# One HGRN2 chunk at a time against chunks in pairs: level products of 256 tokens in two PSUM banks, the banks shared out anew

## The chip, the cores and the metric

The kernel runs on one core of one Trainium2 chip. The metric is the device time of one execution in microseconds (us), as the median over several runs. Five engines work side by side, each through its own instructions in order: TensorE (PE; PEld is its weight load), VectorE (DVE), ScalarE (ACT), GpSimd (POOL) and SyncE (SP), which issues nearly all DMAs. Products are written to PSUM, which has eight banks of 512 fp32 values per partition.

## The reference

One layer of a hybrid trunk: 1024 tokens and 16 meta tokens ahead of them, width 1024. One input projection feeds three mixers, whose outputs (384 + 384 + 256 wide) go through one output projection, a layer norm, a squared-ReLU MLP (hidden width 4096) and a second layer norm. The change touches the first mixer, HGRN2, with 6 heads of 64:

```python
zf = f_raw;  q = silu(q_raw);  v = i_raw
log_f = logaddexp(log_sigmoid(zf), log(lb) + log_sigmoid(-zf))     # log of the forget gate
k = (1 - lb) * sigmoid(-zf)
# per chunk, with G = cumsum(log_f) over the tokens of the chunk
o_inter = (q * exp(G)) @ state
scores[t, s] = sum_k q[t, k] * exp(G[t, k] - G[s, k]) * k[s, k]     # s <= t
o = o_inter + scores @ v
state = exp(G_last) * state + (k * exp(G_last - G)).T @ v
...
o = rms_norm(o) * norm_w * silu(g_raw)
h = layer_norm(ALPHA * h + concat(y_a, y_b, y_c) @ w_out)
ff = square(relu(h @ w_mlp_in)) @ w_mlp_out
h = layer_norm(ALPHA * h + ff)
```

## The kernel before

**Precision and products.** Most products are "three-part" ones: `mm3` (L107 to L110) splits each fp32 operand into a rounded `hi` (ScalarE, L100) and the rest `lo` (VectorE, L87) and issues hi x hi, lo x hi and hi x lo. The small products of the mixers are plain fp32 and take two passes each on PE.

**Order.** The kernel is a list of units (Python functions that issue some instructions). `run(*streams)` interleaves several lists in proportion. A scheduler then fixes, when the kernel is compiled, the order of the instructions on every engine, going by the program order and by what it estimates to be ready; on the chip an engine takes its instructions strictly in that order, and a wait holds up all that stands behind it.

**Stages.** First the v and dt columns, then the projections for S5, HGRN2 and Mamba (tiles of 264 + 264 + 512 columns, or 512), during which S5 runs. Then `run(gt + xt[4:] + zt[0], hg_units(first half), mamba prefixes)`: the remaining projections are the filler under HGRN2's chunks 0 to 3. Then the output projection of the first 512 tokens (`wout_units`, `accumulate`: products into the bank `o`, added to `acc` by DVE), beside the rest of Mamba chunks 0 to 3. Then the layer norm of tiles 0 to 3 (`norm1`, `layer_norm`), the transposes of the result into `h1` (`h1_transpose`: four 128x128 transposes per bank, split into `h1_0_0` by ACT and `h1_0_1` by DVE), and the first MLP pieces (`pre`) as filler under HGRN2 and Mamba of chunks 4 to 7. Then the output projection of the second half, four MLP passes by Strassen's scheme (`strassen_units`: banks of `pg` for the products 2, 5 and 3, banks of `p_sc` and `p_o` for the products 1, 6, 7 and 4), the rest of the MLP, and the last norm.

**HGRN2.** A chunk is 128 tokens. `hg_prep` makes A = q * decay (block-diagonal over two heads), B = k and QK. Seven levels h = 1, 2, ..., 64 follow: `hg_level` multiplies B with A (L766: three fp32 products into one bank `pm_sc`), copies the valid entries into P (for h < 32 a masked copy on DVE, L777; for 32 and 64 plain copies on ACT, L773), and then `hg_decay` multiplies A and B by the decay F of the next longer blocks (L81, DVE; two halves of A, then B, then F). `hg_out` makes the output and the new state, `hg_norm` the RMS norm, the transposes, the gate and the store to `mixA_d`. In the first half two sets of buffers let chunk c+1 run five units behind chunk c; in the second half there is one set, and chunks follow each other.

**PSUM.** Eight banks: `g` 3 (projections, MLP up, Strassen), `sc` 2 (levels, Mamba scores and states, S5, h1 transposes, half of Strassen's products), `tr` 1 (transposes and others), `o` 2 (outputs, accumulations, the rest).

## Time and profile before

| | us |
|---|---|
| median of 3 runs | 1262.05 (1261.17 to 1262.55) |
| profiled execution | 1263.05, its span 1260.9 |
| PE busy | 1234.8 of the span |
| DVE, ACT, POOL busy | 816.6, 533.7, 22.9 |
| PE idle, 250 to 322 (HGRN2, first half) | 2.1 |
| PE idle, 378 to 413 (output projection begins) | 4.4 |
| PE idle, 441 to 458 (first layer norm) | 2.5 |

The span is one core's; the device time adds about 2 us around it. "Idle" is the length of a stretch less the time in which PE ran a product. A product's duration in the trace overlaps the next one's, so distances between starts, not durations, tell what a product costs in a row of them. A row of waits names the line that waited, then what it waited for.

### The profile page before, as it was taken

The page shows a single profiled execution, that of the slowest core. Times are in us where ns is not written, and L with a number is a line of the kernel's source. Part 1 is how long each engine was busy: PE and PEld are TensorE (multiplying, and loading weights), DVE is VectorE, ACT ScalarE, POOL GpSimd, SP SyncE. Part 2 cuts the span into 40 slices and gives each one's busy share as a digit, 9 for nine tenths or more (in the row PEclk, how much of TensorE's full clock was granted, in tenths as well). Part 3 has the DMA queues.
Part 4 walks back from the last instruction along what each step waited for, and adds up shares of the span by engine and source line. Part 5 has one row for each costly group of instructions (what it writes and reads, how often), then busy time and mean ns, then how long its engine had stood idle before and what let it go on. Part 6 is the DMA issues. An engine that isn't in the chain of part 4 may idle for free.

```text
span 1260.9 us, 17709 instructions
## 1 busy us (share of the span) xinstructions
PE 1234.8 (98%) x6488; PEld 1034.4 (82%) x6488; DVE 816.6 (65%) x1763; ACT 533.7 (42%) x1176; POOL 22.9 (2%) x30
## 2 busy tenths in 40 slices
PE   8999999999998999999999999999999999999997
PEld 8988888688886888888888888888888888787886
DVE  7915865688757797767554854936729459844525
ACT  5242233433774465445444334324334343533611
POOL 0000000000000000000000000000000000200002
PEclk9999999999999999999999999999999999999999
DMA  8152334224457222323154331220311312532501
GB/s 280 38 156 77 70 110 118 101 73 136 153 168 240 70 89 70 92 82 106 54 164 134 116 109 51 66 85 25 103 40 50 94 49 81 170 101 85 166 1 67
DMA packets 82935, 127.40 MB, mean 101 GB/s; under 512 B 8480, under 2 KB 34592, under 8 KB 82848
## 3 DMA queue, kind: packets, MB, share of 16 engines
q1 hardware_dynamic: 82848, 126.27, 32.3%
q8 instruction: 51, 0.84, 0.3%
q14 instruction: 36, 0.29, 0.1%
HBM read 105.44 MB, written 19.75 MB: 99 GB/s over the span
## 4 chain that ended last, share of the span: by engine, by line
PE 88%; DVE 7%; ACT 2%; DMA 2%; issue 1%; POOL 0%; POOLq 0%; SPq 0%; DVEq 0%; ACTq 0%
PE pg L109 16%; PE pg L108 16%; PE pg L110 16%; PE pm_o L108 7%; PE pm_o L110 7%; PE pm_o L109 7%; PE pm_sc L766 3%; PE pm_sc L108 1%; PE pm_sc L110 1%; PE pm_sc L109 1%; PE pv L108 1%; PE pv L109 1%; PE pv L110 1%; PE pm_o L789 1%; PE pm_sc L963 1%
## 5 line engine op out<-in xcount | busy, mean ns | idle before, releaser
L87 DVE TENSOR_TENSOR lo<-raw,hi 128x512 fp32r<-128x512 f32 x264 | 181.3, 692 | 157.7 <-ACT hi L100 155.1
L100 ACT CAST hi<-raw 128x512 fp32r<-128x512 f32 x264 | 162.8, 620 | 281.3 <-PE pg L109 145.0
L109 PE MATMUL pg<-h,hi 128*128 128x512 f32 (+1 forms) x544 | 206.7, 380 | 0.9 <-DVE h L87 0.9
L108 PE MATMUL pg<-h,hi 128*128 128x512 f32 (+1 forms) x544 | 207.2, 382 | 0.0
L110 PE MATMUL pg<-h,lo 128*128 128x512 f32 (+1 forms) x544 | 206.7, 380 | 0.0
L109 PEld LDWEIGHTS pg<-h,hi 128*128 128x128 f32 x544 | 102.3, 188 | 21.3 <-DVE h L87 1.1
L110 PEld LDWEIGHTS pg<-h,lo 128*128 128x128 f32 x544 | 102.2, 188 | 20.5
L108 PEld LDWEIGHTS pg<-h,hi 128*128 128x128 f32 x544 | 102.1, 188 | 20.3
L108 PE MATMUL pm_o<-hi,fh 128*128 128x512 f32 (+1 forms) x296 | 117.3, 396 | 1.2 <-ACT fh L100 1.2
L110 PE MATMUL pm_o<-hi,fl 128*128 128x512 f32 (+1 forms) x296 | 114.3, 387 | 0.0
L109 PE MATMUL pm_o<-lo,fh 128*128 128x512 f32 (+1 forms) x296 | 114.2, 387 | 0.0
L84 DVE TENSOR_TENSOR acc<-acc,pm_o 128x512 f32<-128x512 f32 (+1 forms) x87 | 59.0, 679 | 59.0 <-PE pm_o L110 57.9
L108 PE MATMUL pg<-x0h,hi 128*128 128x264 f32 (+1 forms) x264 | 84.9, 322 | 0.0
L109 PE MATMUL pg<-x0l,hi 128*128 128x264 f32 (+1 forms) x264 | 84.3, 319 | 0.0
L110 PE MATMUL pg<-x0h,lo 128*128 128x264 f32 (+1 forms) x264 | 83.9, 318 | 0.0
L108 PE MATMUL pg<-x1h,hi 128*128 128x512 f32 x168 | 66.5, 396 | 0.0
L110 PE MATMUL pg<-x1h,lo 128*128 128x512 f32 x168 | 66.2, 394 | 0.0
L108 PEld LDWEIGHTS pm_o<-hi,fh 128*128 128x128 f32 x296 | 55.7, 188 | 12.8 <-ACT fh L100 2.0
L109 PE MATMUL pg<-x1l,hi 128*128 128x512 f32 x168 | 66.1, 394 | 0.0
L110 PEld LDWEIGHTS pm_o<-hi,fl 128*128 128x128 f32 x296 | 55.5, 188 | 11.9 <-DVE fl L87 0.4
L109 PEld LDWEIGHTS pm_o<-lo,fh 128*128 128x128 f32 x296 | 55.8, 188 | 10.5
L109 PE MATMUL pm_o<-lo,h 128*128 128x512 f32 x128 | 50.5, 395 | 2.5 <-DVE lo L87 2.5
(383 smaller groups left out, 2383.1 us busy)
## 6 DMA issues: line engine op xcount, KB each, us to landing
...
```

The source lines that it names most:

```text
L84: e.tensor_tensor(out=out, in0=a, in1=b, op=ALU.add)
L87: e.tensor_tensor(out=out, in0=a, in1=b, op=ALU.subtract)
L100: S.copy(hi, src)
L108: PE.matmul(out, wh, xh, start=start, stop=False, **kw)
L109: PE.matmul(out, wh, xl, start=False, stop=False, **kw)
L110: PE.matmul(out, wl, xh, start=False, stop=stop, **kw)
L766: PE.matmul(ps[:, ct * 128:ct * 128 + 128].rearrange("p (g b l) -> p g b l", g=2, l=h), hb["B"][:, ct, :], Av, start=True, stop=True, skip ...
L789: PE.matmul(o, hb["P"][:, h, :], v[:, h * 64:h * 64 + 64], start=False, stop=False, skip_group_check=True)
L963: PE.matmul(o[:, h], gd[:, h], tri_le, start=(h == 0), stop=(h == 2), skip_group_check=True)
```

## The change

HGRN2 takes two chunks at a time, 256 tokens in lock step. The level tile `pm_sc` is one tile of two banks, written by six products in one burst; A, P and F are twice as wide; the keys are scaled and decayed in place in `kf` (no B of their own); `hg_decay` now stands ahead of the copy out of PSUM; the norm, the load of the gate and the store of mixA are done once per pair. One set of buffers serves both halves. 22 units per half replace 40. PSUM becomes `g` 2, `sc` one tile of two banks for the levels alone, `tr` 2 (and all that had used `sc` apart from the levels), `o` 2. Mamba's `y` has two buffers instead of three. The small tile vt[0] moves to another pool, and the rsqrt tiles are 12 wide.

```diff
-    psG = ctx.enter_context(tc.tile_pool(name="psG", bufs=3, space=PSUM, reuse_waits="tile"))
+    psG = ctx.enter_context(tc.tile_pool(name="psG", bufs=2, space=PSUM, reuse_waits="tile"))
...
-    def p_sc():
-        return pm("sc", 2)
+    def p_two():
+        return psM.tile([128, 2, 512], F32, tag="sc", name="pm_sc", bufs=1)
     def p_tr():
-        return pm("tr", 1)
+        return pm("tr", 2)
+    p_sc = p_tr
...
+    def hg_gates(c0, n):
+        HB["F"][1] = zf[:, :, c0:c0 + n]
+        HB["B"] = kf[:, :, c0:c0 + n]
         for ct in range(3):
-            scale(hb["B"][:, ct, :n], kf[:, ct, c0:c0 + n], oml[:, ct:ct + 1])
+            scale(HB["B"][:, ct], HB["B"][:, ct], oml[:, ct:ct + 1])
...
+    def hg_level(h):
         nbc = 64 // h
-        ps = p_sc()
-        for ct in range(3):
-            Av = hb["A"][:, ct].rearrange("p g (b two l) -> p g b two l", two=2, l=h)[:, :, :, 1, :]
-            PE.matmul(ps[:, ct * 128:ct * 128 + 128].rearrange("p (g b l) -> p g b l", g=2, l=h),
-                      hb["B"][:, ct, :], Av, start=True, stop=True, skip_group_check=True)
+        ps = p_two()
+        for i in range(2):
+            cs = slice(128 * i, 128 * i + 128)
+            for ct in range(3):
+                Av = HB["A"][:, ct, :, cs].rearrange("p g (b two l) -> p g b two l", two=2, l=h)[:, :, :, 1, :]
+                PE.matmul(ps[:, i, ct * 128:ct * 128 + 128].rearrange("p (g b l) -> p g b l", g=2, l=h),
+                          HB["B"][:, ct, cs], Av, start=True, stop=True, skip_group_check=True)
...
+        hg_decay(h, W2, True)
         if h >= 32:
...
-            V.copy_predicated(dst, m.rearrange("p h (b l) -> p h b l", l=h), src)
-        hg_decay(hb, h, 128, True)
+            m = m.unsqueeze(1).unsqueeze(1).to_broadcast([128, 2, 6, nbc, h])
+            V.copy_predicated(dst, m, src)
...
-    def hg_units(cs, lag):
+    def hg_units(cs):
         us = []
-        for st in range(lag * (len(cs) - 1) + 10):
-            for i, c in enumerate(cs):
-                if 0 <= st - lag * i < 10:
-                    us.append(lambda c=c, j=st - lag * i: hg_unit(c, j))
+        for c in cs[::2]:
+            us.append(lambda c=c: hg_prep(c))
+            us += [lambda j=j: hg_level(1 << j) for j in range(7)]
+            us += [lambda c=c: hg_out(c), lambda c=c: hg_out(c + 1), lambda c=c: hg_norm(c)]
         return us
...
-        y = mb.tile(sh6, F32, tag="y", name="y", bufs=3)
+        y = mb.tile(sh6, F32, tag="y", name="y", bufs=2)
...
-            bank[t] = p_sc() if t % 2 == 0 else p_o()
+            bank[t] = p_tr() if t % 2 == 0 else p_o()
...
-    wk = hg_buffers(2)
+    wk = hg_buffers()
...
-    hgb = hg_units(h1_, 10)
+    hgb = hg_units(h1_)
```

In the rows that follow an engine's instructions stand in their order: line, operation, out<-in with the tile's number, shape, and in brackets the engines or DMA queues that it waits for.

*A level on DVE, first half.* Before, around the level h=2 of chunk 0 (A0, B0; QK1 and B1 belong to the chunk that runs behind it):

```order
L777 COPY_PREDICATED P0_2240<-kc_64,pm_sc_2349 128x192x2 [waits PE_49]
L81 TENSOR_TENSOR A0_2237<-A0_2237,F2_0_2241 64x3x32x2 x2
L81 TENSOR_TENSOR B0_2238<-B0_2238,F2_0_2241 128x96x2
L81 TENSOR_TENSOR F16_0_2244<-F8_0_2243 128x24 [waits DVE_49]
L81 TENSOR_TENSOR QK1_2253<-qr_453,B1_2252 128x384 [waits Activation_49]
L81 TENSOR_TENSOR F32_0_2245<-F16_0_2244 128x12 [waits DVE_49]
L90 SCALAR_TENSOR_TENSOR sig_2537<-sig_2537,pk_63,pg_2512 128x512 [waits DMAHW3_49]
L777 COPY_PREDICATED P0_2240<-kc_64,pm_sc_2428 128x96x4 [waits PE_49]
L81 TENSOR_TENSOR A0_2237<-A0_2237,F4_0_2242 64x3x16x4 x2
L81 TENSOR_TENSOR B0_2238<-B0_2238,F4_0_2242 128x48x4
```

The masked copy out of PSUM comes first, then the multiplies on A0 and B0 for the next level. After, the same level of the first pair (A is `A_2237`, B is the tile `kf_452`):

```order
L90 SCALAR_TENSOR_TENSOR sig_2562<-sig_2562,pk_63,pg_2537 128x512 [waits DMAHW6_49,Activation_49]
L81 TENSOR_TENSOR A_2237<-A_2237,F2_2239 64x3x64x2 [waits PE_49]
L81 TENSOR_TENSOR A_2237<-A_2237,F2_2239 64x3x64x2
L81 TENSOR_TENSOR kf_452<-kf_452,F2_2239 128x3x64x2
L782 COPY_PREDICATED P_2238<-kc_64,pm_sc_2407 128x384x2
L81 TENSOR_TENSOR F16_2242<-F8_2241 128x48 [waits DVE_49]
L81 TENSOR_TENSOR F2_2239<-zf_451 128x384 [waits DVE_49]
```

The multiplies are twice as wide and come first; the copy, which frees the two-bank tile for the next burst, comes last, and work of other units stands ahead of the group.

*The output projection's first sums.* PE before, `pm_o_4026` and `pm_o_4067` being the two first accumulations:

```order
L110 MATMUL pm_o_4026<-hi_4011,h1_0_1_3933 128x512
L108 MATMUL pm_o_4067<-hi_3981,h1_0_0_3932 128x512
L109 MATMUL pm_o_4067<-lo_3982,h1_0_0_3932 128x512
L110 MATMUL pm_o_4067<-hi_3981,h1_0_1_3933 128x512
L108 MATMUL pm_o_4067<-hi_3991,h1_0_0_3932 128x512
L109 MATMUL pm_o_4067<-lo_3992,h1_0_0_3932 128x512
L108 MATMUL pm_o_4026<-hi_4021,h1_0_0_3932 128x512 [waits Activation_49]
L110 MATMUL pm_o_4067<-hi_3991,h1_0_1_3933 128x512
L108 MATMUL pm_o_4067<-hi_4001,h1_0_0_3932 128x512
```

The second one has a bank of its own and starts without a wait, in turns with the first. PE after (`pm_o_3864` and `pm_o_3905`; `pm_tr_3807` takes the transposes of Mamba's `y` of chunk 0):

```order
L108 MATMUL pm_o_3864<-hi_3859,h1_0_0_3770 128x512 [waits Activation_49]
L109 MATMUL pm_o_3864<-lo_3860,h1_0_0_3770 128x512 [waits DVE_49]
L110 MATMUL pm_o_3864<-hi_3859,h1_0_1_3771 128x512
L108 MATMUL pm_o_3905<-hi_3819,h1_0_0_3770 128x512 [waits DVE_49]
L109 MATMUL pm_o_3905<-lo_3820,h1_0_0_3770 128x512
L1023 MATMUL pm_tr_3807<-kc_64,y_3243 128x128 [waits DVE_49,PE_49]
L110 MATMUL pm_o_3905<-hi_3819,h1_0_1_3771 128x512
L1023 MATMUL pm_tr_3807<-kc_64,y_3243 128x128 [waits DVE_49]
```

The second accumulation waits for DVE. What stands in DVE's queue there:

```order
L81 TENSOR_TENSOR A_4194<-A_4194,zf_451 64x3x128 [waits Pool_49]
L90 SCALAR_TENSOR_TENSOR rsm_3793<-rs_t_3797,rs_y_3798 128x2 [waits DVE_49]
L90 SCALAR_TENSOR_TENSOR acc0_3775<-acc0_3775,pm_o_3864 128x512 [waits PE_49]
L90 SCALAR_TENSOR_TENSOR y_3243<-y_3243,rsm_3793,pk_63 128x192 [waits DVE_49]
L90 SCALAR_TENSOR_TENSOR y_3243<-y_3243,rsm_3793,pk_63 128x192
L81 TENSOR_TENSOR kf_452<-kf_452,zf_451 128x3x128
L782 COPY_PREDICATED P_4195<-kc_64,pm_sc_4522 128x768 [waits Pool_49]
L81 TENSOR_TENSOR y_3621<-pm_tr_3609,ea_2277 128x384 [waits DVE_49,PE_49]
L87 TENSOR_TENSOR h1_0_1_3771<-pm_tr_3807,h1_0_0_3770 128x3x128 [waits Activation_49]
L84 TENSOR_TENSOR y_3621<-y_3621,pm_o_3608 128x384 [waits DVE_49]
```

The first accumulation's sum into `acc0` frees the bank that the second needs; `y_3621` (chunk 2), which frees the banks of `pm_tr_3609` and `pm_o_3608`, stands behind the level's `kf` multiply and its masked copy.

*The first layer norm.* `acc2` and `acc3` are the tiles 2 and 3 under the norm. PE before, from the last filler products to the transposes of tile 3 (L1110):

```order
L110 MATMUL pg_4779<-h1_0_0_3932,lo_4774 128x256
L108 MATMUL pg_4779<-h1_0_0_3932,hi_4773 128x256
L109 MATMUL pg_4779<-h1_0_1_3933,hi_4773 128x256
L110 MATMUL pg_4779<-h1_0_0_3932,lo_4774 128x256
L988 MATMUL pm_tr_4819<-S2_2233,xb_4629 128x192 [waits Activation_49]
L988 MATMUL pm_tr_4819<-S2_2233,xb_4629 128x192
L1110 MATMUL pm_sc_4615<-kc_64,acc3_3940 128x128 [waits DVE_49,PE_49]
L1110 MATMUL pm_sc_4615<-kc_64,acc3_3940 128x128 x3
L1110 MATMUL pm_sc_4622<-kc_64,acc3_3940 128x128 [waits PE_49]
```

The 18 products that end here stand between the transposes of tile 2 and of tile 3. PE after, from the transposes of tile 2 (`pm_tr_4419`, `pm_tr_4426`) on:

```order
L1107 MATMUL pm_tr_4419<-kc_64,acc2_3777 128x128 [waits DVE_49,PE_49]
L1107 MATMUL pm_tr_4419<-kc_64,acc2_3777 128x128 x3
L1107 MATMUL pm_tr_4426<-kc_64,acc2_3777 128x128 [waits PE_49]
L1107 MATMUL pm_tr_4426<-kc_64,acc2_3777 128x128 x3
L769 MATMUL pm_sc_4546<-A_4194,kf_452 128x128 [waits DVE_49]
L769 MATMUL pm_sc_4546<-A_4194,kf_452 128x128 x2
L1107 MATMUL pm_tr_4451<-kc_64,acc3_3778 128x128 [waits DVE_49,PE_49]
L1107 MATMUL pm_tr_4451<-kc_64,acc3_3778 128x128 x3
L1107 MATMUL pm_tr_4458<-kc_64,acc3_3778 128x128 [waits PE_49]
L1107 MATMUL pm_tr_4458<-kc_64,acc3_3778 128x128 x3
L769 MATMUL pm_sc_4546<-A_4194,kf_452 128x128 x3
L110 MATMUL pg_4628<-h1_0_0_3770,lo_4617 128x256 [waits DVE_49]
```

Between tile 2 and tile 3 there is now the first half of the burst for h=4 (`pm_sc_4546`), and the projection products (`pg_4628`) follow after tile 3. DVE before, from tile 3's statistics to the end of its norm (L90 into `acc3`):

```order
L1085 BN_AGGR mv_4600<-bst_4597 128x2
L87 TENSOR_TENSOR lo_4774<-raw_4771,hi_4773 128x512 [waits DMAHW6_49]
L96 TENSOR_SCALAR rs_h_4603<-mv_4600 128x1 [waits DVE_49]
L90 SCALAR_TENSOR_TENSOR acc3_3940<-acc3_3940,mv_4600,gb_3925 128x1024
L87 TENSOR_TENSOR h1_0_1_3933<-pm_sc_4583,h1_0_0_3932 128x4x128 [waits Activation_49]
L87 TENSOR_TENSOR h1_0_1_3933<-pm_sc_4590,h1_0_0_3932 128x4x128 [waits Activation_49]
L90 SCALAR_TENSOR_TENSOR rs_t_4604<-rs_y_4605,rs_h_4603 128x1 [waits DVE_49,Activation_49]
L87 TENSOR_TENSOR fl_4734<-sig_4760,fh_4733 128x256
L90 SCALAR_TENSOR_TENSOR lrs_4602<-rs_t_4604,rs_y_4605 128x1 [waits DVE_49]
L87 TENSOR_TENSOR lo_4944<-raw_4941,hi_4943 128x512 [waits DMAHW7_49]
L90 SCALAR_TENSOR_TENSOR lnm_4611<-mv_4600,lrs_4602 128x1 [waits DVE_49]
L90 SCALAR_TENSOR_TENSOR acc3_3940<-acc3_3940,lrs_4602,gb_3925 128x1024
```

DVE after, over the same work:

```order
L1082 BN_AGGR mv_4436<-bst_4433 128x2
L81 TENSOR_TENSOR A_4194<-A_4194,F2_4196 64x3x64x2
L96 TENSOR_SCALAR rs_h_4439<-mv_4436 128x1 [waits DVE_49]
L90 SCALAR_TENSOR_TENSOR acc3_3778<-acc3_3778,mv_4436,gb_3763 128x1024
L87 TENSOR_TENSOR h1_0_1_3771<-pm_tr_4419,h1_0_0_3770 128x4x128 [waits Activation_49]
L87 TENSOR_TENSOR h1_0_1_3771<-pm_tr_4426,h1_0_0_3770 128x4x128 [waits Activation_49]
L90 SCALAR_TENSOR_TENSOR rs_t_4440<-rs_y_4441,rs_h_4439 128x1 [waits DVE_49,Activation_49]
L81 TENSOR_TENSOR kf_452<-kf_452,F2_4196 128x3x64x2
L90 SCALAR_TENSOR_TENSOR lrs_4438<-rs_t_4440,rs_y_4441 128x1 [waits DVE_49]
L782 COPY_PREDICATED P_4195<-kc_64,pm_sc_4534 128x384x2
L90 SCALAR_TENSOR_TENSOR lnm_4447<-mv_4436,lrs_4438 128x1 [waits DVE_49]
L90 SCALAR_TENSOR_TENSOR acc3_3778<-acc3_3778,lrs_4438,gb_3763 128x1024
```

The level h=2 of the pair (A, `kf`, and the copy out of `pm_sc_4534`, L782) now stands among the norm's instructions, ahead of tile 3's last one; the conversions `lo_4617` and `lo_4623`, two of the kind that stood among them before, come behind it.

145 lines of the change are left out of this document (67 added, 78 removed).

## The prediction

> **What bounds the kernel now.** I read the page's first part and its chain first: they say which engine is full and whether its own work makes the end.
>
> ```profile
> PE 1234.8 (98%) x6488; PEld 1034.4 (82%) x6488; DVE 816.6 (65%) x1763; ACT 533.7 (42%) x1176; POOL 22.9 (2%) x30
> PEclk9999999999999999999999999999999999999999
> PE 88%; DVE 7%; ACT 2%; DMA 2%; issue 1%; POOL 0%; POOLq 0%; SPq 0%; DVEq 0%; ACTq 0%
> ```
>
> TensorE (PE) is busy 98% of the span at a full granted clock, and VectorE (DVE) 65%. The change leaves the number of products as it is, so the time can move only by PE's idle time and by what switching between kinds of products costs. The 150 or so DVE instructions that it saves count only where DVE is what PE waits for. So the second view is the list of PE's waits.
>
> ```profile
> PE pv L108 <- ACT x0h L100: 4.6, 1, 4.6
> PE pm_o L109 <- DVE lo L87: 2.5, 1, 2.5
> PE pm_tr L1026 <- DVE y L90: 1.9, 2, 1.3
> PE pm_sc L1110 <- DVE acc L90: 1.6, 1, 1.6
> PE pm_sc L766 <- DVE B L81: 1.3, 4, 0.4
> PE pg L109 <- DVE h L87: 0.9, 1, 0.9
> PE pm_sc L766 <- DVE P L777: 0.8, 2, 0.6
> PE pm_tr L475 <- ACT W L476: 0.3, 1, 0.3
> ```
>
> Columns: total us, how often, longest. L766 is the HGRN2 level product itself: it costs 2.1 us of waiting in all, so a perfect pairing could not win more than that there. The third view, busy time in chosen stretches, shows where the rest lies (the first number after the colon is the length of the stretch).
>
> ```profile
> 250.00:290.00 40.00, 38.49 (x266) 33.30 (x265) 35.96 (x106) 13.86 (x36) 0.00 (x0) 1.00 0.24 73
> 290.00:322.00 32.00, 31.38 (x209) 26.87 (x210) 24.96 (x61) 15.88 (x41) 0.00 (x0) 1.00 0.39 123
> 378.00:413.00 35.00, 30.59 (x154) 24.58 (x152) 26.86 (x62) 18.27 (x48) 0.00 (x0) 1.00 0.72 225
> 441.00:458.00 17.00, 14.52 (x111) 13.25 (x109) 16.64 (x36) 11.42 (x35) 0.00 (x0) 1.00 0.15 48
> 458.00:483.00 25.00, 24.06 (x194) 22.91 (x194) 22.35 (x58) 11.52 (x32) 0.00 (x0) 1.00 0.35 101
> ```
>
> PE idles 1.51 + 0.62 = 2.1 us in the first half's HGRN2 (250 to 322), 4.4 us at the start of the output projection (378 to 413), 2.5 us around the first layer norm (441 to 458) and 0.9 us where chunk 4's levels run (458 to 483). In 441 to 458 DVE is busy 16.64 of 17 us: there DVE is the bound, and anything put into its queue there is paid in full.
>
> **The change, part by part.** *Fewer switches.* A level burst stands between projection products.
>
> ```profile
> 540.30 0.40 PE L110 MATMUL pg<-h,lo 128*128 128x512 f32 x1
> 540.53 0.85 PE L766 MATMUL pm_sc<-A,B 128*128 128x128 f32 x6
> 541.13 0.48 PE L108 MATMUL pg<-h,hi 128*128 128x512 f32 x1
> 541.45 0.40 PE L109 MATMUL pg<-h,hi 128*128 128x512 f32 x1
> ```
>
> Products of this width start 0.23 us apart (540.30 to 540.53); the burst takes 0.60 us to the next start, and the first product after it needs 0.32 instead of 0.23. Coming back costs 0.09 us. In the order of all products PE comes back 137 times before and 118 times after the change: 19 x 0.09 = -1.7 us. Bounds: -1.0 (half of it hidden under waits that stay) and -2.5 (28 bursts fewer, all counted).
>
> *The level loop.* Its prices:
>
> ```profile
> L81 DVE TENSOR_TENSOR A<-A,F 64x192 f32<-64x192 f32 x96 | 33.8, 353 | 3.1 <-PE pm_sc L766 1.8
> L81 DVE TENSOR_TENSOR A<-qr,zf 64x384 f32<-64x384 f32 x16 | 8.8, 551 | 5.6 <-PE pm_o L790 5.4
> L81 DVE TENSOR_TENSOR QK<-qr,B 128x384 f32<-128x384 f32 x8 | 4.4, 553 | 0.1
> 462.88 1.02 DVE L777 COPY_PREDICATED P<-kc,pm_sc 128x384 f32<-128x384 int32 x1
> 469.43 0.57 DVE L777 COPY_PREDICATED P<-kc,pm_sc 128x384 f32<-128x384 int32 x1
> L87 DVE TENSOR_TENSOR lo<-raw,hi 128x512 fp32r<-128x512 f32 x264 | 181.3, 692 | 157.7 <-ACT hi L100 155.1 <-PE pm_tr L475 2.0
> ```
>
> A doubled decay multiply is priced by the 384-wide rows: 0.55 us, three per level. No row has a 768-wide masked copy: twice 0.57 is the upper bound, and with the fixed part of the multiplies (353 at 192 and 551 at 384 leave 155 ns) it is about 1.0 us; at h=1 from 1.02 to about 1.85. Before, the burst has two one-bank tiles, so the next burst waits only for the three multiplies, and two chunks alternate. After, all six products go into the one two-bank tile; the next burst waits for the multiplies and for the copy, which is issued after them. From burst start to next burst start that is 1.5 (twelve records at 0.1 and the end of the last) + 3 x 0.57 + 1.0 = 4.2 us with nothing else on DVE. In pair 1 the order leaves 1.2 us of burst and 2.6 to 2.9 us of projection between most neighbours, 3.8 to 4.1 us, and often puts one or two 0.69-us conversions (`lo`) into the same DVE gap. Summed place by place I get 0.45, 0.4, 0.25 and 0.3 us in pair 1, 0.15, 0.5 and 0.45 in pair 2, and 0.3 each around the outputs and the norm transposes: 3.3 us for 2.1 before, so +1.2. Bounds: -1.5 (DVE ready nearly everywhere) and +3.5 (each of the ten dense places late by another conversion and its queue).
>
> The Trainium skill, PSUM — Partial Sum Buffer, section "Summary: rules for kernel authors", says to read PSUM while matmuls run from a different bank than the one they write. It speaks against the two-bank tile, which holds both banks until the copy is done. By the rule alone all 24 later bursts would wait out a copy of 1.0 us, 24 us in all; the order puts enough products between most of them, which the traced 0.8 us of waits on P shows to work, so the sum above stays with the places.
>
> *The start of the output projection.* The 2.5-us wait on `lo` (378 to 413) came from a late chain: the last chunk's mixA store, its reload and the conversions. After the change the last pair's transposes stand about 60 products ahead of this stage instead of 40, 4.5 us earlier at 0.23 each. But `y` with two buffers holds py and pf of Mamba chunk 2 in PSUM until `y` of chunk 0 is transposed, so the first two accumulations share one o bank.
>
> ```profile
> L90 DVE SCALAR_TENSOR_TENSOR acc<-acc,pm_o 128x512 f32<-128x512 f32 x26 | 17.8, 684 | 20.6 <-PE pm_o L110 20.5
> ```
>
> The second accumulation waits for the end of the first (0.39 - 0.23), 0.68 for the sum and 0.1 of hand-over, with 0.3 of decay left in the queue: 1.25 us. The gate transposes of chunk 1 then need the bank of pf, which DVE frees after kf (0.55), the h=1 copy (1.85) and y (0.55): 0.8 us more. About 0.95 stays of the `lo` wait (the table load and the squares stand ahead of the last casts on ACT) and 0.2 of the y waits. 3.2 after for 4.4 before: -1.2. Bounds: -3.5 (all covered) and +1.0 (mixA no earlier).
>
> *Around the first layer norm.* This decides. Before, between tile 2's transposes and tile 3's, PE had 18 projection products (452.35 to 454.46) and state products as filler, and idled only for the last 1.59 us:
>
> ```profile
> 451.56 1.03 PE L1110 MATMUL pm_sc<-kc,acc 128*128 128x128 f32 x8
> 452.35 0.36 PE L108 MATMUL pg<-h,hi 128*128 128x256 f32 x1
> 452.55 0.28 PE L109 MATMUL pg<-h,hi 128*128 128x256 f32 x1
> 452.67 0.28 PE L110 MATMUL pg<-h,lo 128*128 128x256 f32 x1
> ...
> 454.46 0.28 PE L110 MATMUL pg<-h,lo 128*128 128x256 f32 x1
> 456.98 1.06 PE L1110 MATMUL pm_sc<-kc,acc 128*128 128x128 f32 x8 [1.59 <-DVE acc L90]
> 451.96 1.27 DVE L90 SCALAR_TENSOR_TENSOR acc<-acc,mv,gb 128x1024 f32<-128x1024 f32 x1
> 453.16 1.28 DVE L87 TENSOR_TENSOR h<-pm_sc,h 128x512 fp32r<-128x512 f32 x2
> 454.48 0.42 DVE L87 TENSOR_TENSOR fl<-sig,fh 128x256 fp32r<-128x256 f32 x1
> 455.56 1.28 DVE L90 SCALAR_TENSOR_TENSOR acc<-acc,lrs,gb 128x1024 f32<-128x1024 f32 x1
> ```
>
> After, pair 2 of level h=2 sits there: two A multiplies, kf and the copy, 3 x 0.55 + 1.0 = 2.7 us of a full DVE queue, and the burst of h=4 is written on PE between the transposes of tile 2 and tile 3, behind that copy. The filler went: those products now need the weight conversion `lo_4617`, which stands on DVE behind tile 3's norm. From tile 2's transposes to tile 3's I count the old 4.63 us plus 1.55 (kf, copy) less 1.1 (fl 0.42, lo 0.69, now later) = 5.1; PE has 0.65 us of work in it: 4.4 idle for 1.6, +2.8. Then `fl` and three `lo` (0.35 + 3 x 0.6) stand ahead of tile 3's h1, for whose tr bank the next Mamba product waits: +0.95. The first tiles' waits grow from 0.9 to 1.6 (+0.7), one later burst waits 0.35, and the 0.9 of 458 to 483 goes, its levels being spread. Sum +2.8 + 0.95 + 0.7 + 0.35 - 0.9 = +3.9. Bounds: -0.5 (PE gets there as late as DVE) and +6.0 (every A multiply paid as well).
>
> *Two g banks instead of three; shared tr banks.* ACT empties these banks, among its conversions.
>
> ```profile
> L100 ACT CAST hi<-raw 128x512 fp32r<-128x512 f32 x264 | 162.8, 620 | 281.3 <-PE pg L109 145.0
> ```
>
> A short projection tile (24 products, 264 or 256 wide, 0.12 us each as from 452.55 to 452.67) gives ACT 2.9 us to empty the other bank, where it had 5.8. ACT is busy 42%, and needs 0.6 us for a copy; in Strassen I find the reused bank free each time (a sum ends 1.2 us after its last product, with 4 to 5 products of another bank between). Cover: those products; without it each miss costs about 0.5. Bounds 0 and +2.5; I take +0.7, a few misses at the size of the one-bank wait on W (0.3). That wait itself goes with the second tr bank: -0.3.
>
> *Costed at nothing.* Keys in place, the shared qk tile, 12-wide rsqrt and the halved number of norms are off the path: about 150 DVE instructions fewer, under the same products. SP issues 8 DMAs fewer; the one mixA store per pair delays only an even chunk, which is read two stages later. The wider POOL memsets (0.75 to about 1.5 us for P) run under the last gate projections, some 13 us; without that cover they would delay the first second-half burst by at most 1.5.
>
> ```profile
> L697 POOL MEMSET P<- 128x768 f32 x3 | 2.2, 746 | 6.4 <-PE pm_o L540 6.3
> ```
>
> **The sum**, against the profiled execution's 1263.05 us (span 1260.9): -1.7 + 1.2 - 1.2 + 3.9 + 0.7 - 0.3 = +2.6, so 1265.65 there. The profiled execution lies 1.0 above the median of the runs (1262.05); taken off, that is 1264.65. New waits are easier overlooked than found, so I say 1265.
>
> **Rivals.** *Faster.* The scheduler's order is met in time: DVE reaches the h=2 copy before PE needs the bank. For it: DVE work falls by about a tenth of its instructions, and 65% is far from full. Against: 16.64 of 17 us. It decides when the level and norm terms together stay under +0.7: -1.7 - 1.2 - 0.3 + 0.7 + 0 = -2.5, 1259.5; at their lower bounds (-1.5 and -0.5) the time is 1257.5. The Trainium skill, VectorE: DVE Perf Modes, section "The TRN2 errata — SBUF-src ops pay a fixed extra latency per instruction", says that one wide operation pays its fixed cost once and many narrow ones each time; the 353 and 551 ns agree, and were DVE the bound throughout, halving the level instructions would win. It is not, by the page's 65%.
>
> *No change.* The norm term is half as large (+2.0), since some filler product reaches PE between: 1262.7.
>
> *Much slower.* The two g banks bind: 24 tiles of 264 and 8 of 256 columns, each late by half a conversion (0.3) = 9.6 instead of 0.7: 1273. It decides from about 10 late tiles. Against it: ACT's 42%.
>
> The Trainium skill, TensorE: Matmul & The Clock Gate, section "A second HAM failure mode: psum-queue depth-cycling", says that many micro-idles at PSUM banks make the clock fall. Here the clock row shows 9 in all slices in spite of idle times up to 4.6 us; I give it 2 in 100, inside this rival.
>
> **Chances.** Forecast (slower by 0.2 to 0.6%) 0.42, much slower 0.08, no change 0.32, faster 0.18. What a measurement of this kernel can tell from no change is about 0.2%, 2.5 us: 1259.5 to 1264.6 counts as the same. Range: the low end takes in no change and reaches the rival's deciding point, 1259.5; the high end takes the norm term at +6 and the levels near +3, 1269.5.
>
> **What would show it.** Right: the waits list names L769 (the level product) with P or kf and over 4 us in all, the largest single one near the second layer-norm transposes; PE busy in that stretch falls while DVE stays full; the `lo` wait of 2.5 falls below 1.5 and a wait of pm_o on acc of about 1.2 appears. Wrong: waits of L769 under 2 us, or pg waiting for ACT in many places.

## The result, and the profile after

| | before | changed |
|---|---|---|
| median in us | 1261.64 (4 runs, 1261.17 to 1262.55) | 1269.91 (4 runs, 1268.41 to 1271.50) |
| ratio | | 1.0065, interval 1.0050 to 1.0081 |
| profiled execution, its span | 1263.05, 1260.9 | 1268.41, 1266.6 |
| mean granted clock of the runs | 0.998 | 0.991 to 0.994 |

The change made the kernel slower by 8.3 us. The forecast was 1265.0, 3 us slower, with a range up to 1269.5: the right side, but less than half the size, and the measured median lies just above the range. The profiled execution of the changed kernel is the fastest of its four, 1.5 us below their median; the profiled one of before, which is not among its four, lies 1.4 us above theirs. So between the two traces the span is only 5.7 us longer. The first part of the page and its chain, after:

```profile
PE 1236.5 (98%) x6488; PEld 1038.6 (82%) x6488; DVE 800.4 (63%) x1581; ACT 528.2 (42%) x1144; POOL 24.9 (2%) x27
PEclk9999999999999989999999999999999999999999
PE 85%; DVE 9%; DMA 3%; ACT 1%; issue 1%; SPq 0%; POOL 0%; POOLq 0%; DVEq 0%; ACTq 0%
```

DVE has 182 instructions less and 16 us less work, and the time is not shorter for it. PE is busy 1.7 us longer with the same 6488 products: there is an 8 in the clock row. PE's waits after (total us, how often, longest):

```profile
PE pm_sc L769 <- DVE P L782: 5.5, 4, 4.6
...
PE pg L108 <- ACT uch L633: 2.9, 1, 2.9
PE pm_o L108 <- ACT hi L100: 1.8, 1, 1.8
PE pm_o L108 <- DVE acc L90: 1.2, 1, 1.2
...
PE pm_sc L769 <- DVE F L81: 0.9, 1, 0.9
PE pg L109 <- DVE h L87: 0.6, 1, 0.6
...
PE pm_o L109 <- DVE lo L87: 0.2, 1, 0.2
```

The first, fourth and last row are as forecast: the burst h=4 behind the masked copy at the layer norm (4.6 us for 4.4 forecast), the second sum on `acc` (1.25 for 1.25), the wait on `lo` down to 0.2. The second row was not forecast. It stands at the very start, where the first S5 projection (tiles of 264, 264 and 512 columns) runs. Stretches there, before and then after (length; busy us of PE, PEld, DVE, ACT, POOL; clock; DMA share; GB/s):

```profile
50.00:54.00 4.00, 4.00 (x25) 3.53 (x24) 3.90 (x8) 1.62 (x3) 0.00 (x0) 1.00 0.00 2
54.00:56.00 2.00, 2.00 (x11) 1.65 (x10) 2.00 (x5) 1.23 (x4) 0.00 (x0) 1.00 0.00 0
```

```profile
50.00:54.00 4.00, 1.26 (x11) 1.04 (x9) 3.93 (x9) 1.94 (x4) 0.00 (x0) 0.98 0.01 2
54.00:56.00 2.00, 1.83 (x4) 1.49 (x5) 2.00 (x5) 0.39 (x2) 0.00 (x0) 0.50 0.00 0
```

The timeline of the changed kernel there, PE and then ACT:

```profile
50.98 0.28 PE L110 MATMUL pg<-x0h,lo 128*128 128x264 f32 x1
54.16 0.79 PE L108 MATMUL pg<-x1h,hi 128*128 128x512 f32 x1 [2.91 <-ACT uch L633]
54.76 0.63 PE L109 MATMUL pg<-x1l,hi 128*128 128x512 f32 x1
55.18 0.63 PE L110 MATMUL pg<-x1h,lo 128*128 128x512 f32 x1
...
52.03 0.25 ACT L868 ACTIVATE me<-mx 128x54 f32<-128x54 f32 x1 [6.03 <-DVE mx L84]
52.30 1.28 ACT L869 ACT_TABLE_LOAD   x1
53.59 0.25 ACT L869 ACTIVATE me<-me 128x54 f32<-128x54 f32 x1
53.75 0.65 ACT L633 COPY uch<-pg 128x264 f32<-128x264 f32 x2
```

ACT idles 6 us, but in its queue an activation of `mb_dt` (L868) and its table load stand ahead of the copies that empty the two g banks, and that activation waits for DVE, which is full with the S5 parameters. The copies come at 53.75. In the kernel before they came no earlier, behind the same activation:

```profile
52.35 0.25 ACT L871 ACTIVATE me<-mx 128x54 f32<-128x54 f32 x1 [6.16 <-DVE mx L84]
...
54.06 0.65 ACT L630 COPY uch<-pg 128x264 f32<-128x264 f32 x2
```

With three banks PE filled the third meanwhile; with two it stands for 2.91 us. And the granted clock is at 0.50 behind it: the 512-wide products start 0.42 us apart (54.76 to 55.18) instead of 0.23, until about 57. The same happens at the layer norm:

```profile
456.00:459.00 3.00, 0.53 (x5) 0.30 (x3) 2.97 (x7) 1.71 (x6) 0.00 (x0) 1.00 0.00 0
459.00:462.00 3.00, 0.91 (x4) 0.91 (x5) 3.00 (x5) 0.00 (x0) 0.00 (x0) 0.66 0.00 0
462.00:465.00 3.00, 3.00 (x16) 3.00 (x16) 2.94 (x6) 1.10 (x2) 0.00 (x0) 0.50 0.20 57
465.00:468.00 3.00, 3.00 (x21) 3.00 (x21) 2.87 (x5) 1.28 (x4) 0.00 (x0) 0.70 0.57 206
```

The clock falls during the 4.56-us wait and stays at 0.50 for some 7 us.

To see where time is gained or lost for good, one can take the n-th product of one kind (those into `pg`, say) in both traces and subtract the starts: the shift. It stays constant where the two kernels run alike. From the changed kernel, its second trace (e7), and the kernel before with two g banks (e4), each against the kernel before, in us:

| place, by the time of before | changed | changed, again | before, two g banks |
|---|---|---|---|
| first S5 product, 45.5 | -0.1 | -0.6 | 0.0 |
| behind the first S5 projection, 62.6 | +4.5 | +6.1 | +4.8 |
| before the first HGRN2 burst, 224.8 | +3.8 | +5.5 | +4.8 |
| end of the output projection's first part, 440 | +4.2 | +5.3 | +3.7 |
| MLP under the second half, 663 | +4.9 | +4.9 | +3.8 |
| last part, 1200 | +5.9 | +5.9 | +4.9 |

The start alone loses 4.6 us (4.5 + 0.1) in the changed kernel; the 440 us in which HGRN2 and the norm lie add 1.1 in one trace and take 0.6 off in the other; the rest, mostly the Strassen passes, adds 1.0.

One place in the traced execution of before is not typical of that kernel, and every shift behind it is too small by it. The first wait of the output projection on `lo`, in before, then in e8 and in e14, two runs below whose kernels are the one before up to there:

```profile
390.37 0.50 PE L109 MATMUL pm_o<-lo,h 128*128 128x512 f32 x1 [2.50 <-DVE lo L87]
```

```profile
389.20 0.50 PE L109 MATMUL pm_o<-lo,h 128*128 128x512 f32 x1 [1.72 <-DVE lo L87]
```

```profile
388.87 0.50 PE L109 MATMUL pm_o<-lo,h 128*128 128x512 f32 x1 [1.22 <-DVE lo L87]
```

From there to 440 us e8 and e14 gain 1.4 and 1.3 us on the traced execution of before, about as much as that execution lies above its median. Against a usual execution the changed kernel thus loses about 1.4 us more behind 400 us than the table shows (an estimate from these two traces).

### The profile page after: what moved, and what is told of

The parts are those of the page before. It is cut to its first block, busy times and chain, and to the rows that moved or that the text cites. A ratio compares the mean times of both kernels' runs of the same rounds, so it can differ in the third digit from the quotient of the medians.

```text
span 1266.6 us, 17497 instructions
## 1 busy us (share of the span) xinstructions
PE 1236.5 (98%) x6488; PEld 1038.6 (82%) x6488; DVE 800.4 (63%) x1581; ACT 528.2 (42%) x1144; POOL 24.9 (2%) x27
## 4 chain that ended last, share of the span: by engine, by line
PE 85%; DVE 9%; DMA 3%; ACT 1%; issue 1%; SPq 0%; POOL 0%; POOLq 0%; DVEq 0%; ACTq 0%
PE pg L108 16%; PE pg L110 15%; PE pg L109 15%; PE pm_o L108 8%; PE pm_o L110 8%; PE pm_o L109 8%; PE pm_sc L769 3%; DMA xr<-xT 1%; PE pm_tr L108 1%; PE pm_tr L109 1%; PE pm_tr L110 1%; PE pm_o L794 1%; DVE P L782 1%; PE pm_o L795 1%; DMA raw<-mixC_d 1%
## 5 line engine op out<-in xcount | busy, mean ns | idle before, releaser
L108 PE MATMUL pm_o<-hi,h 128*128 128x512 f32 x128 | 51.3, 401 | 3.1 <-ACT hi L100 1.8
```

Source lines behind the costliest of these rows:

```text
L108: PE.matmul(out, wh, xh, start=start, stop=False, **kw)
```

## The experiments

The theory: the two g banks carry the loss, by one place where ACT is held up, by the clock behind it, and by small delays in Strassen. The rival, from the prediction: the level's copy ahead of the norm carries it. Ratios are to the kernel before, run beside each.

### Levels of pair 2 later (e1), and a third bank for one projection (e2)

```diff
-    for f in mbb[:2] + hgb[:5]:
+    for f in mbb[:2] + hgb[:2]:
...
-    run(pre[:cu2], hgb[5:], mbb[2:])
+    run(pre[:cu2], hgb[2:], mbb[2:])
```

> The changed kernel, but only the preparation and level h=1 of pair 2 are put ahead of the MLP pieces; levels h=2 to h=8 come later, between the products. Theory A (the wait of the h=4 burst on the h=2 copy near the layer norm costs its 4.56 us of idle AND a halved clock for some us behind it): the idle between tile 2's and tile 3's transposes falls to 1.5 to 2 us, the granted clock stays at 1.00 there, and the time falls by about 3 + 2.5 = 5.5 us, from 1269.9 to about 1264.5. Theory B (only the idle counts, the clock loss is an accident of the run): 1266.9. Theory C (the work put later only waits elsewhere): 1269 to 1270, with a new idle behind the layer norm.

Measured: 1269.39, 1.0059 (1.0045 to 1.0073), the changed kernel's own time. The 4.56 us became waits of 2.09, 0.24 and 1.37 at the same place, and the clock fell all the same (0.50 from 465 to 468). Theory C of this run: the work waits elsewhere.

```diff
-            ps = pg()
+            ps = p_two()[:, 0] if spare and n == HALF else pg()
...
-        gemm_ch(ct, TB3, ev_u(uch))
+        gemm_ch(ct, TB3, ev_u(uch), ct == 0)
```

> The changed kernel, but the third block of the first S5 projection goes into one bank of the idle two-bank level tile, so it need not wait for one of the two g banks. Theory A (the 2.91-us wait at 51.3 us costs itself and about 1.5 us of products at half clock behind it): the wait on uch vanishes, the clock stays at 1.00 from 44 to 70 us, and the time falls by 2.9 + 1.5 = 4.4 us, to about 1265.5. Theory B (the clock there does not depend on the wait): falls by 2.9, to 1267.0. Theory C (the wait is hidden by what follows, ACT being late anyway): 1269.5.

Measured: 1270.83, 1.0070 (1.0058 to 1.0083): no gain, and none of the three theories. The wait moved ten microseconds on and grew:

```profile
PE pg L108 <- ACT uch L633: 4.8, 1, 4.8
```

The second projection's copies wait for the store of the first one's `uch` tile, whose landing at 66 us is late in all kernels; its own third block needs a third bank as well.

### More work for PE in the idle time (e3)

```diff
+    def extra(n):
+        ps = p_o()
+        for i in range(n):
+            PE.transpose(ps[:, i % 4 * 128:i % 4 * 128 + 128], acc[2][:, i % 8 * 128:i % 8 * 128 + 128], ident)
...
-    for f in wu + sum([[lambda t=t: norm1(t), lambda t=t: h1_transpose(t)] for t in h0], []):
+    for f in wu + sum([[lambda t=t: norm1(t), lambda t=t: h1_transpose(t)] + [lambda: extra(20)] * (t == 2) for t in h0], []):
```

> The changed kernel with 20 further transposes of 0.1 us each, whose result nobody reads, in PE's order right behind tile 2's transposes, so that they fall into the 4.56-us idle ahead of the h=4 burst. It does 2 us more work. Theory A (an idle of more than about 3.4 us halves the clock): the idle shrinks to about 2.2 us, the clock stays at 1.00 from 456 to 468 us, the 8 transposes of tile 3 take 0.8 us instead of 1.7, and the time falls by 2 to 2.5 us, to about 1267.5, though nothing is waited for less. Theory B (the clock falls for another reason, or the slow products are hidden by DVE's queue): 1269.9, no change.

Measured: 1269.92 in the median (1267.67 to 1270.73), 1.0059 (1.0045 to 1.0073). In the trace the idle time is 1.39 us, the clock stays at 1.00 through the norm, and the shift falls from +4.4 to +4.15 across it where the changed kernel's rises by 0.6. Against that trace 0.9 us is gained, but in e7 and e12, two more traces with the whole 4.56-us wait and the halved clock, the shift falls by 0.4 and 0.5 there, more than in e3. So no gain is shown, and the median shows none: theory B. (The run's own trace had 4.2 us of wait at the start.)

### Two g banks in the kernel before (e4)

```diff
-    psG = ctx.enter_context(tc.tile_pool(name="psG", bufs=3, space=PSUM, reuse_waits="tile"))
+    psG = ctx.enter_context(tc.tile_pool(name="psG", bufs=2, space=PSUM, reuse_waits="tile"))
```

> The kernel before, with two g banks instead of three and nothing else. Theory A (the g-bank part of the change costs the wait of 2.9 us at the start and 1.5 us of half clock, and nothing in other places): slower by 4.4 us, about 1266.0, with a wait of pg on ACT uch of 2.9 us in the waits list and the clock at 0.5 near 55 us. Theory B (only the wait): 1264.5. Theory C (the two banks bind in many places, each short projection tile late by 0.3): 1271 or more. Theory D (hidden): 1261.6.

Measured: 1267.97, 1.0051 (1.0037 to 1.0065), slower by 6.1 (theory A of e4 had 4.4, with nothing for Strassen). One bank taken away, with nothing of the pairing, costs three quarters of what the whole change costs. Its waits:

```profile
PE pg L108 <- ACT uch L630: 3.1, 1, 3.1
...
PE pm_o L109 <- DVE lo L87: 1.0, 1, 1.0
```

The shift is +4.8 from 60 us on, falls by 1.1 at the output projection, and rises by 1.05 from 790 us on, in the Strassen passes. The fall is no gain of this kernel: e8 and e14, with three banks, gain 1.4 and 1.3 us at the same place on the same trace. The two other terms make 5.9 us, for 6.1 measured. In those passes no wait is long enough for the list. Three products in a row before, and the same three with two banks:

```profile
789.55 0.39 PE L110 MATMUL pg<-hi,fl 128*128 128x512 f32 x1
789.77 0.39 PE L108 MATMUL pg<-hi,fh 128*128 128x512 f32 x1
790.00 0.39 PE L109 MATMUL pg<-lo,fh 128*128 128x512 f32 x1
```

```profile
793.36 0.39 PE L110 MATMUL pg<-hi,fl 128*128 128x512 f32 x1
793.61 0.50 PE L108 MATMUL pg<-hi,fh 128*128 128x512 f32 x1
793.94 0.39 PE L109 MATMUL pg<-lo,fh 128*128 128x512 f32 x1
```

At 793.61 the first product into a reused bank keeps the next one 0.33 us away instead of 0.23. Three such make a step of about 0.33 in the shift, and it takes three such steps, near 800, 880 and 1050 us: together the 1.05.

### The banks given back (e5, e6), and the changed kernel again (e7)

e5 is e2 with the third block of both projections in the level tile (`True` for `ct == 0`). e6 takes every third projection tile from it wherever no level runs:

```diff
     def pg():
+        n_pg[0] += 1
+        if spare[0] and n_pg[0] % 3 == 0:
+            return p_two()[:, 0]
         return psG.tile([128, 512], F32, tag="g", name="pg")
```

> The changed kernel, with the third block of both of the first two S5 projections in a bank of the idle two-bank level tile (the run that did it for the first projection alone only moved the wait to the second, where it was 4.8 us). Theory A (the two g banks at the start cost the idle and the slow clock behind it, 4.6 us by the shift of the products behind that place): no wait of pg on uch over 0.5 us, clock 1.00 from 44 to 70 us, time 1269.9 - 4.6 = 1265.3. Theory B (the start is slack for what follows, the norm region sets the time): 1269 or more. Theory C (the wait moves once more, to the third projection): 1268 to 1270.

> The changed kernel, but wherever no level runs (the stages ahead of the first level, between the halves, and the MLP behind the last) every third projection tile goes into a bank of the two-bank level tile, so that these stages have three banks again as before. Theory A (the g banks carry the whole loss: 4.6 us at the start and 1.05 us in the Strassen passes, where a product that reuses a bank starts 0.1 us late): 1269.9 - 5.6 = 1264.3, and the products of the MLP stand at a constant shift against the kernel before. Theory B (only the start): 1265.3. Theory C (the loss is in the levels and at the norm): above 1268.

> The changed kernel itself, once more, for a second trace and its spread. Theory A (its runs differ by how far the clock falls in the two long waits): the granted clock of the runs lies between 0.990 and 0.995, the runs with the lower clock are the longer ones, about 1 us for each 0.001, and the median is 1269 to 1270.5. Theory B (the spread has nothing to do with the clock): no such order among the runs.

Measured: e5 1264.49, 1.0015 (1.0007 to 1.0024); e6 1265.04, 1.0022 (1.0012 to 1.0033); e7 1269.02, 1.0051 (1.0038 to 1.0064). With its bank back at the start alone the kernel is 4.5 us faster than e7 (4.6 by theory A of e5). The stretch of e5 that answers to the one above:

```profile
50.00:54.00 4.00, 4.00 (x21) 3.37 (x21) 3.83 (x11) 1.28 (x2) 0.00 (x0) 1.00 0.00 0
54.00:56.00 2.00, 2.00 (x11) 1.65 (x10) 2.00 (x5) 1.67 (x6) 0.00 (x0) 1.00 0.02 4
```

In e6 the Strassen passes add nothing more (shift +0.50 at 671 us, +0.43 at 1095), so the 1.05 is the third bank too. But then it loses 2.45 us at one place: the wait at the last MLP stage grew from 1.2 to 2.05 us, and the clock fell behind it (0.50 from 1102 to 1104). Of the runs of e7 the two at a clock of 0.993 are the longest (1269.12 and 1269.89; the others, at 0.994, 1268.40 to 1269.02); in e3, e5 and e6 too the run with the lowest clock (0.993, 0.991, 0.991) is the longest (1270.73, 1266.45, 1268.48). In e1 and e10 it is not, so the clock is only a part of the spread.

### What an idle time costs (e8)

```diff
+    def pause(n):
+        tc.strict_bb_all_engine_barrier()
+        for _ in range(n):
+            add(V, idle, idle, idle)
+        tc.strict_bb_all_engine_barrier()
```

> The kernel before, with five pauses of different length put into its MLP part, where TensorE is otherwise full: all engines meet, VectorE does 1, 3, 6, 12 or 18 short dependent additions, all engines meet again. This measures what an idle time of TensorE costs there. Theory A (an idle time over about 3.4 us halves the granted clock for some us behind it, a shorter one does not): the short pauses show a clock of 1.00 behind them, the long ones 0.50 for 3 to 7 us. Theory B (the clock falls with the busy share over a longer stretch): no fall behind a single pause. Theory C (any idle time over 1 us): a fall behind all of them.

Measured: the shortest pause was already 4.42 us, so what a shorter one costs this run does not show. All five pulled the clock down:

| pause, idle us | shift it added | beyond the idle time |
|---|---|---|
| 4.42 | 6.84 | 2.4 |
| 5.05 | 7.56 | 2.5 |
| 5.73 | 8.79 | 3.1 |
| 7.25 | 9.81 | 2.6 |
| 8.79 | 10.56 | 1.8 |

Stretches around the first and the last pause:

```profile
822.00:824.00 2.00, 0.45 (x2) 0.03 (x1) 0.92 (x2) 0.00 (x0) 0.00 (x0) 1.00 0.00 0
824.00:826.00 2.00, 0.00 (x0) 0.00 (x0) 0.00 (x0) 0.00 (x0) 0.00 (x0) 0.64 0.60 208
826.00:829.00 3.00, 2.13 (x5) 1.70 (x6) 1.48 (x3) 1.86 (x3) 0.00 (x0) 0.50 0.75 255
...
832.00:835.00 3.00, 3.00 (x14) 2.45 (x14) 1.35 (x2) 0.83 (x2) 0.00 (x0) 1.00 0.75 226
...
1194.00:1196.00 2.00, 0.67 (x3) 0.19 (x1) 1.17 (x4) 0.00 (x0) 0.00 (x0) 1.00 0.00 0
1196.00:1198.00 2.00, 0.00 (x0) 0.00 (x0) 1.76 (x8) 0.00 (x0) 0.00 (x0) 0.66 0.00 0
...
1203.00:1206.00 3.00, 2.54 (x6) 2.01 (x7) 2.14 (x4) 2.27 (x4) 0.00 (x0) 0.50 0.74 254
```

The clock falls 2 to 5 us after the idle time began, not at a fixed distance, and is back 3 to 6 us after the products go on; behind the first pause ten of them run 0.43 us apart. A wait of PE of 4.4 us or more thus cost itself plus 1.8 to 3.1 us where products follow that are bound by PE. That rest is about half of the time in which products ran at the halved clock: 3.4 to 5.9 us by the trace.

### Everything given back (e9)

e9 joins the third bank ahead of the levels and in Strassen (not in the last stage), a third bank for the output projection's sums, and e3's 20 transposes:

```diff
-        ps = p_o()[:, 0:nc_]
+        n_o[0] += 1
+        ps = (p_two()[:, 0] if o_sp[0] and n_o[0] % 3 == 0 else p_o())[:, 0:nc_]
```

> The changed kernel with four additions: every third projection tile ahead of the first level, and every third one of the Strassen passes, goes into a bank of the idle level tile (in the last MLP stage no longer, where this lengthened a wait to 2.05 us); every third sum of the output projection's first part does so too; and the 20 unread transposes behind tile 2's norm. Theory A (the losses are the g banks, the shared o bank and the clock behind the norm's long wait): 1269.4 less 4.6 (start) less 1.05 (Strassen) less 0.5 to 1.2 (pm_o on acc) less 0.9 (norm): about 1262, level with the kernel before. Theory B (only the g banks): 1264. Theory C (the output projection is bound by what ACT converts, so that a further o bank only lengthens the wait on hi): 1263 to 1264, the wait on hi longer by as much as the one on acc is shorter.

Measured: 1262.15, 1.0004 (0.9996 to 1.0013): the kernel before, within 0.1%, as theory A had it, all runs at a clock of 0.997 to 0.999. Its waits:

```profile
PE pm_sc L774 <- DVE P L787: 2.5, 5, 1.4
PE pm_o L108 <- ACT hi L100: 1.9, 1, 1.9
...
PE pm_tr L1009 <- DMA sz<-sz_d: 0.9, 1, 0.9
```

The wait on `acc` is gone, that on `uch` too, and the clock stays at 1.00 up to the last 6 us. Of the 7 us, 4.5 are the bank at the start (e5); what the other banks and the 20 transposes brought each is not shown.

### More work for DVE (e10), and the copy first (e11)

```diff
+    def extra(t):
+        for j in range(2):
+            V.tensor_reduce(out=dv[:, j:j + 1], in_=acc[t], axis=AX.X, op=ALU.add)
```

> The changed kernel with two sums over 128x1024 on VectorE, about 1.1 us each, that nobody reads, behind the norm of tile 2, where TensorE idles 4.56 us. Theory A (VectorE's queue sets the pace from the layer norm to about 480 us, so that TensorE's idle time there is only its shadow): the whole 2.2 us is paid, 1269.4 + 2.2 = 1271.6, and the shift of the products behind 500 us grows by 2. Theory B (the 4.56 us are one late wait, and later slack on VectorE takes up more work): below 1270.4.

Measured: 1268.99, 1.0059 (1.0046 to 1.0072), no longer than the changed kernel, where theory A had 1271.6. At the place itself the wait took it all:

```profile
PE pm_sc L769 <- DVE P L782: 7.7, 4, 6.8
```

From 440 to 671 us the shift grew by 1.8 us, where it changed by +0.6, -0.4 and -0.5 in the changed kernel, e7 and e12: 1.2 to 2.3 us of the 2.2 are paid there. But from 671 us on this run gained it back, because the products of the MLP's down part stood 0.2284 us apart instead of 0.2315. That was the tile `dv` (below): e12 has the tile without the sums, and from 671 us to the end it gains as much (shift -1.3 in both). By the medians e10 is only 0.0004 above e12, 0.5 us, less than the two intervals can tell apart; so that the sums are paid is read from the traces alone.

```diff
         dst = HB["P"].rearrange("p i h (b two l) -> p i h b two l", two=2, l=h)[:, :, :, :, 1, :]
-        hg_decay(h, W2, True)
         if h >= 32:
...
             V.copy_predicated(dst, m, src)
+        hg_decay(h, W2, True)
```

> The changed kernel with the masked copy of each level put back ahead of the level's decay multiplies, as it was before the change. Theory A (a burst waits for the one two-bank tile, so the earlier copy frees it 1.7 us earlier): the waits of the level product on P fall from 5.5 to about 3 us, the one at the norm from 4.56 to about 3, and the time falls by 1 to 2 us. Theory B (the next burst then waits as long for the multiplies, since A and the keys are needed too): waits on P are replaced by waits on A, F or kf of the same length, time unchanged within 0.5. Theory C (what is slack in the first half is lost by the multiplies being late): slower by up to 2.

Measured: 1268.75, 1.0059 (1.0047 to 1.0070), not to be told from the changed kernel. The waits on P are gone, and waits on the keys have taken their place (3.8 us, the longest 3.2, beside 1.3 on tile 3's norm): mostly theory B.

### Where the operands lie (e12 to e17)

```diff
+    dv = small.tile([128, 2], F32, tag="dv", name="dv", bufs=1)
+    G.memset(dv, 0.0)
```

The tile is not used. It moves the tiles on one side of SBUF (the weights `hi` and `lo`, `fh` and `fl`, `h1_0`) by 32 bytes; those on the other side (`h1_1`, further `fh`) stay. e12 has it in the changed kernel, e13 in e9, e14 in the kernel before; e15 is e13 with 96 bytes, e16 with 224, e17 is e12 with 224. The distances in the table are those of the addresses in the compiled kernels, which a profile doesn't hold.

> The changed kernel with one unused tile of 8 bytes per partition, set to zero once on GpSimd, so that the tiles allocated behind it lie 8 bytes further on; it is the control for the run with more VectorE work, which had the same tile. Theory A (the products of the MLP's down part from 671 us on ran at 0.2284 instead of 0.2315 us apart in that run because of where their operands lie, which hid the price of the two sums): the same pace here, and a time 2.0 us below the changed kernel's, 1267. Then the two sums cost about 2 us, and VectorE sets the pace at the norm. Theory B (the pace came from the sums' own shift in time): 0.2315 as before and 1269, and the two sums cost nothing in the end.

> The kernel with more banks and the 20 transposes, with the same 8-byte tile. Theory A (the place of the operands): 1262.2 - 2.0 = 1260.2, below the kernel before by 1 to 2 us. Theory B: 1262.2, unchanged.

> The kernel before, with the same 8-byte tile. Theory A (the place of the operands): 1261.3 - 2.0 = 1259.3, the products of the down part 0.2284 us apart instead of 0.2313. Theory B: 1261.3, unchanged.

> The kernel with more banks and the 20 transposes, with an unused tile of 96 bytes instead of 8. The weights' tiles (hi, lo) then lie at 38240 and up, and the second half's rows (h1_1) at 174048: their distance is 640 modulo 2048, a multiple of 128. In the four kernels so far it was 1056 (kernel before) and 736 (changed), both 32 modulo 64, with the MLP's products 0.2302 to 0.2322 us apart, 704 (changed, 8 bytes) with 0.2284 to 0.2324, and 1024 (before, 8 bytes) with 0.2267. Theory A (full pace needs a distance that is a multiple of 128): 0.2267 throughout the MLP, 1262.2 - 8 = 1254. Theory B (a multiple of 256 or more is needed): between 1257 and 1261. Theory C (the distance does not matter, something else moved): 1260 or more.

> The same with 224 bytes: the distance is 512 modulo 2048. Theory A (a multiple of 128): as the run with 96 bytes, 1254. Theory B (a multiple of 256 or 512): 1254 here, and slower with 96. Theory C: 1260 or more.

> The changed kernel itself with the unused tile of 224 bytes, so that the distance of the operands is 512 modulo 2048, as in the run of 1253.9 us. Theory A (the change's loss has nothing to do with the operands' place): 1254 + 7.5 = 1261.5, as far above the kernel before with 8 bytes (1254.0) as the changed kernel is above the kernel before. Theory B (part of the loss is one of place): less than 5 us above 1254.0.

| run | kernel | weights to `h1_1`, bytes modulo 256 | median | ratio |
|---|---|---|---|---|
| before | before | 32 | 1261.6 | 1 |
| e14 | before | 0 | 1253.98 | 0.9940 (0.9927 to 0.9952) |
| e7 | changed | 224 | 1269.02 | 1.0051 (1.0038 to 1.0064) |
| e12 | changed | 192 | 1268.42 | 1.0055 (1.0042 to 1.0069) |
| e17 | changed | 0 | 1261.99 | 1.0007 (0.9998 to 1.0015) |
| e9 | e9 | 224 | 1262.15 | 1.0004 (0.9996 to 1.0013) |
| e13 | e9 | 192 | 1259.88 | 0.9986 (0.9977 to 0.9995) |
| e15 | e9 | 128 | 1262.18 | 1.0006 (0.9997 to 1.0015) |
| e16 | e9 | 0 | 1253.91 | 0.9939 (0.9927 to 0.9952) |

The same stretch of 80 us in the MLP's last part (the number behind PE's busy time counts its products), first of the kernel before, then of e14:

```profile
1120.00:1200.00 80.00, 80.00 (x345) 64.29 (x344) 37.14 (x56) 39.11 (x67) 0.00 (x0) 1.00 0.40 122
```

```profile
1120.00:1200.00 80.00, 79.97 (x353) 65.83 (x352) 36.05 (x54) 39.38 (x68) 0.00 (x0) 1.00 0.33 106
```

And of e15 and e16:

```profile
1120.00:1200.00 80.00, 80.00 (x346) 64.53 (x344) 37.11 (x55) 39.59 (x67) 0.00 (x0) 1.00 0.38 120
```

```profile
1120.00:1200.00 80.00, 79.97 (x353) 65.81 (x352) 37.16 (x55) 39.43 (x67) 0.00 (x0) 1.00 0.35 109
```

All at a clock of 1.00 and PE full, but 353 products where the distance is 0, against 345 and 346. Theory B of e15 and e16 (a multiple of 256 or 512) is borne out by the three kernels with distance 0 against the others; e15's own number under it, 1257 to 1261, was missed by 1. Theory A of e12 was right in the pace and wrong in the time (1267 for 1268.42), that of e13 right (1260.2 for 1259.88), that of e14 far too small (1259.3 for 1253.98). For the question of this study it matters that the change's loss isn't one of place: at distance 0 the changed kernel stands 8.0 us above the kernel before (e17, theory A, and e14), as at the old distances, and with its banks given back and the 20 transposes 0.1 us below it (e16 and e14).

## Why the prediction was wrong, step by step

**Two g banks, +0.7 with bounds 0 and +2.5: the step that failed.** In the traced run they cost 4.6 us at the start (2.9 of idle, 1.5 at half clock, the rest in starting again) and 1.0 in Strassen, 5.6 in all; taken away alone, in e4, the third bank cost 6.1 of the 8.3. The step gave ACT 2.9 us to empty a bank and set against it that ACT is "busy 42%". A share says nothing of the order: at 50 us ACT was idle and could not copy, since a waiting instruction stood ahead in its queue. The row was in the trace of before: ACT's activation `me` waited 6.16 us for DVE, and the copies of `uch` came at 54.06, 3 us after the second tile's last product; the third bank hid it. And "in Strassen I find the reused bank free each time" did not follow from the step's own numbers: 4 to 5 products of 0.23 us are 0.9 to 1.15 us, less than the 1.2 in which the sum ends. In e4 a reused bank costs 0.1 us a time, which is below what the list of waits shows.

**The clock, 2 in 100.** The clock row of before showed 9 in spite of idle times up to 4.6 us, and I took that for a rule. Those 4.6 us lie at the very start of the span; elsewhere before had none over 2.5. Both long waits of the changed kernel halved the clock. By the traced run this cost about 1.5 us at the start and about 2.5 at the norm (tile 3's eight transposes took 1.70 us instead of 0.79, the burst halves likewise). The two traced executions are 5.4 us apart in device time, the medians 8.3; of the difference 1.4 belong to the traced execution of before, above its median, and 1.5 to that of the changed kernel, below its own. Two of the other three runs of the changed kernel had a lower clock than the traced one's 0.994 (0.992 and 0.991), the third, of 1270.24, did not; so the clock explains this in part at most, and only the first run has a trace.

**Around the first layer norm, +3.9.** The idle time of the main piece came as forecast, 4.56 for 4.4, but by luck. The masked copy ahead of the burst took 1.85 us where the term had 1.0, and from tile 2's transposes to tile 3's it was 6.3 us for 5.1; PE's own work in there took 1.7 us for 0.65, most of it at half clock, so the difference came out the same. The pieces behind it (+0.95, +0.35) did not come, as PE, at half clock, arrived late itself, and the -0.9 of the later levels became -1.4. Idle time from 440 to 650 rose by 1.3 in all (3.97 to 5.27). DVE is busy for nearly all of the time from 440 to 468. There PE's idle time could be cut up (e1) or filled with work (e3) without a gain, and work added to DVE was paid in the trace of e10, though not in its median.

**Fewer switches, -1.7.** It is larger. The projection and output products themselves, from start to next start and without the idle time, take 0.75 us less from 225 to 440 and 2.4 less from 440 to 650: about -3.2, beyond my bound of -2.5. The 0.09 for coming back holds (the mean of 103 such products before), but a large product just ahead of small ones also starts the next 0.04 later, which the term left out. This paid for the clock at the norm.

**The level loop, +1.2.** PE's idle time at the levels of the first half did not grow: 2.05 us for 2.1 before and 3.3 forecast. The copy's price was right for h=4 to h=16 (0.97 to 1.00 us) and for h=1, but h=2 takes as long as h=1 (1.85 to 1.93), where the term had 1.0. The trace of before has a row for h=2 on half the width, shown here ahead of the copy at the norm after:

```profile
466.18 1.04 DVE L777 COPY_PREDICATED P<-kc,pm_sc 128x384 f32<-128x384 int32 x1 [0.17 <-PE pm_sc L766]
```

```profile
459.19 1.85 DVE L782 COPY_PREDICATED P<-kc,pm_sc 128x768 f32<-128x768 int32 x1
```

**The output projection, -1.2:** idle 3.83 for 3.2 forecast and 4.4 before. The `lo` wait went down to 0.2 and a wait of 1.8 on `hi` from ACT came: the chain was only partly earlier. In e8 and e14, with the kernel before, this idle time is 3.1, so against those there was no gain at all. **S5's W wait, -0.3:** gone, worth 0.67 by the shift.

Three sums don't come out as written: the places of the level loop add up to 3.1 and not 3.3, "much slower" to 1273.5, and the high end of the range, from the terms that it names, to 1268.5. None of them changes the account.

So the sum against the traced run, +2.6, had its largest term where little was lost and only 0.7 where nearly all was. Of the rivals, "much slower" had the right resource with the wrong picture: one place, a clock and three steps of a third of a microsecond in Strassen, not 32 late tiles.
